# Differential attention inside a two-layer backbone: three score buffers of two banks, queries placed by transfers, norms for two heads at a time

## The chip, the cores and the metric

The kernel runs on one core of a Trainium2 chip. The metric is the device time of one execution in microseconds, the median of several runs. TensorE (PE) multiplies matrices into PSUM, which has eight banks; VectorE (DVE), ScalarE (ACT) and GpSimd (POOL) work element by element; SyncE (SP) issues the transfers. Each engine, SP's queue too, takes its instructions strictly in a fixed order and waits at one whose data or buffer is not ready.

## The reference, cut to what matters

The program is two layers of a diffusion backbone on 512 latent tokens and 256 context tokens. The change touches the differential attention of each layer, four heads, and what is computed beside it. Per head there are two softmax maps, whose difference weighs the values:

```
s = jnp.einsum("bqhmd,bkhmd->bhmqk", q, k) * (B_QK_DIM ** -0.5)      # m = 0, 1; 64 wide
p = jax.nn.softmax(s, axis=-1)
a = p[:, :, 0] - lam * p[:, :, 1]
o = jnp.einsum("bhqk,bkhd->bqhd", a, v)                               # 128 wide per head
yb = rms_norm(o, subln_g) * (1.0 - lam_init)                          # over the 128 of a head
x  = x + g1 * (concat([ya, yb, yc]) @ w_out)
```

Latent queries see all 768 keys; context queries (layer 0 alone) see the 256 context keys. The products `ya` and `yc` of two other mixers are ready before the attention starts, so that part of the product with `w_out` needs nothing of the attention.

## The kernel before, in words

Work is cut into pairs of a head and a block of 256 queries, and each pair into two units of 128 queries. Layer 0 has 4 context pairs and then 8 latent ones (24 units), layer 1 has 8 latent pairs (16 units). Per pair, `q_prep` transposes the queries on PE (tile `pq`), copies them to a rounded high part `qh` (each half of 64 rows is placed twice, by ACT and GpSimd) and subtracts on DVE for the low part `qlz` (L106). Per unit, `scores` computes for each of the two maps the product with the keys (tile `pss`, L822 with the high part, L823 with the low part), its row maximum on DVE (`mx`, L825) and the exponential on ACT (`e`). `combine` forms the difference of the maps on DVE (L841), and on GpSimd `dg` (L842), the term with the norm's epsilon. `transp` turns the result by six PE transposes (`pat`), copied to `ath` by ACT (L858, first four) and DVE (L860, last two). Per pair, `attn_v` multiplies with the values (`po`, L870), copies to `o`, squares it on ACT (`osq`) and adds `dg` on GpSimd (L875). `subln` sums the squares with a matmul by ones (`pr`, L882), takes logarithm and exponential on ACT, scales on DVE (L885) and splits into `yBh` and `yBl`.

The eight PSUM banks hold two `pss` buffers of two banks, three `w` buffers (`pq`, `pat`, `po` and `pr` take turns in them) and one `f` buffer for the filler. The filler is `wout` for the parts `ya` and `yc` (tiles `yACh`, `yACl`; PSUM tile `wo`): two chunks of weights in layer 0, three in layer 1, added to `xT` by DVE (L758). It stands last in the program, but a scheduler orders the instructions of each engine by priority and readiness, and a buffer of a pool is handed out in the order of the program.

After the fillers the main product with `w_out` follows, which reads `yBh` and `yBl`.

Of the kernel before, what the change touches and what calls it, by code (L numbers as in the profile page):

```python
# [16 lines left out]
P = 128  # L17
# [9 lines left out]
QKD = 64  # L27
# [20 lines left out]
FB, WB, EB, QB = 1, 3, 5, 3  # L48
# [28 lines left out]
def tile_backbone(  # L77
# [254 lines left out]
    for l in range(DEPTH):  # L332
# [433 lines left out]
        with ExitStack() as ph:  # L766
# [4 lines left out]

            qlz = [sp.tile([P, 2, 256], F32R, name=f"qlz{x}") for x in range(2)]
            zero = sp.tile([P, 256], F32, name="zero")
            G.memset(zero, 0.0)
            for x in qlz:
                for m in range(2):
                    ms = slice((1 - m) * QKD, (2 - m) * QKD)
                    G.tensor_copy(x[ms, m], zero[ms])
# [6 lines left out]
            def q_prep(n):  # L785
                h, p = pairs[n]
                qh = sp.tile([P, 2, 256], F32R, tag="qh", name="qh", bufs=QB)
                ql = qlz[n % 2]
                pq = ps.tile([P, 256], F32, tag="w", name="pq", bufs=WB)
                for i in range(2):  # L790
                    T.transpose(pq[:, i * P:(i + 1) * P], qt[2 * p + i][:, h * P:(h + 1) * P], ident)
                if n == 0:
                    for m in range(2):
                        for a in range(2):
                            S.copy(qh[a * QKD:(a + 1) * QKD, m], pq[m * QKD:(m + 1) * QKD])
                    for m in range(2):
                        ms = slice(m * QKD, (m + 1) * QKD)
                        sub_lo(ql[ms, m], pq[ms], qh[ms, m])
                else:
                    qn = sp.tile([P, 256], F32R, tag="qn", name="qn", bufs=2)  # L800
                    S.copy(qn, pq)
                    for m in range(2):
                        src = qn[m * QKD:(m + 1) * QKD]
                        for a in range(2):
                            (G.tensor_copy if a else S.copy)(qh[a * QKD:(a + 1) * QKD, m], src)
                    for m in range(2):
                        ms = slice(m * QKD, (m + 1) * QKD)
                        sub_lo(ql[ms, m], pq[ms], qn[ms])
                st["q", n] = (qh, ql)

            def scores(n, i):
# [17 lines left out]
                st[n, i] = (e, sm)  # L829

            def combine(n, i):
# [3 lines left out]
                if i == 0:  # L835
                    st["dg", n] = sp.tile([P, 2, P], F32, tag="dg", name="dg", bufs=3)
                dg = st["dg", n][:, i]
# [7 lines left out]
            def transp(n, i):  # L845
# [5 lines left out]
                for c0 in range(0, nk, 4):  # L851
# [5 lines left out]
                    if c0 == 0:  # L857
                        S.copy(at[osl], pat[:, :cn_])  # L858
                    else:
                        V.tensor_copy(at[osl], pat[:, :cn_])  # L860

            def attn_v(n):
# [8 lines left out]
                o = sp.tile([P, 256], F32, tag="o", name="o", bufs=2)  # L871
                sq = sp.tile([P, 256], F32, tag="osq", name="osq", bufs=2)
                S.copy(o, po)
                S.activation(sq, o, AF.Square)
                G.tensor_add(sq, sq, st["dg", n].rearrange("p a q -> p (a q)"))  # L875
                st["sub", n] = (o, sq)

            def subln(n):
                h, p = pairs[n]
                o, sq = st["sub", n]  # L880
                pr = ps.tile([P, 256], F32, tag="w", name="pr", bufs=WB)
                T.matmul(pr, ones, sq, start=True, stop=True)  # L882
# [3 lines left out]
                ts = slice(p * 256, p * 256 + 256)  # L886
                S.copy(yBh[:, h, ts], o)
                sub_lo(yBl[:, h, ts], o, yBh[:, h, ts])

            first = [(g, i) for g in whole for i in range(2)]  # L890
            if l == 0:
                w0 = wout_w(0, (0,), "pool")
                g, i = first.pop(0)
                wout(0, (0,), w0, [g], ps, "f", FB, (i,))
            q_prep(0)
            nu = len(units)
            for u in range(nu + 8):
# [15 lines left out]
                if 0 <= v < nu and units[v][1] == 1:  # L913
                    subln(units[v][0])

            for mp2 in range(NFILL[l]):
                if mp2 == 0 and l == 0:
                    for g, i in first:
                        wout(0, (0,), w0, [g], ps, "f", FB, (i,))
                else:  # L920
                    wout(mp2, (0,), wout_w(mp2, (0,), "pool"), whole, ps, "f", FB)
# [253 lines left out]
```

## Time and profile before

| | us |
|---|---|
| median of 3 runs | 1602.82 (1602.46 to 1603.99) |
| the profiled execution | 1602.73 |
| its span, first to last instruction | 1600.4 |
| PE busy in it | 1565.2 (98%) |
| DVE busy | 1016.0 (63%) |
| ACT busy | 643.3 (40%) |
| GpSimd busy | 113.3 (7%) |

The shares are means over stages that differ. The attention of layer 0 lies at about 244 to 354 us, that of layer 1 at about 1109 to 1197 us. Elsewhere after the first 100 us, PE is busy nearly without a break. A busy PE is not PE at its best: matmuls overlap, so the distance from one start to the next is what one costs in a dense row.

### The profile page before, as it was taken

Reading aid. Unit: us, or ns where it says so; the run is one execution under the profiler, and the core shown is the slowest. Engines: PE = TensorE matmul, PEld = TensorE weight load, DVE = VectorE, ACT = ScalarE, POOL = GpSimd, SP = SyncE. Lnnn points to the kernel's source line nnn. Section 1 sums busy time; section 2 is a strip of 40 time slices with the busy share of each in tenths; the row PEclk is TensorE's granted clock in tenths of the full one; section 3 lists DMA queues with packets and bytes.
Section 4 is the critical chain, followed back from the end, with each engine's and each line's share of the span. In section 5 each row is a group of like instructions: output and inputs, shape, how many; then the busy total and the mean of one; then the engine's idle time right before and its main releaser. Section 6 shows DMA issues by size and latency. Waiting matters only on the chain.

```text
span 1600.4 us, 21118 instructions
## 1 busy us (share of the span) xinstructions
PE 1565.2 (98%) x8186; PEld 1289.8 (81%) x8186; DVE 1016.0 (63%) x1713; ACT 643.3 (40%) x1115; POOL 113.3 (7%) x128
## 2 busy tenths in 40 slices
PE   6999998999999999999999999999999999999999
PEld 4875776778788888888888887887778888888888
DVE  4497968969999982145444354996977444334433
ACT  5431568762532221124333233255765333123321
POOL 1130124310000000000000000001320000000000
PEclk9999999999999999999999999999999999999999
DMA  7625210015265872116666476642011323332232
GB/s 282 216 68 183 62 54 27 14 40 198 68 196 185 284 257 74 63 66 198 209 192 207 152 272 221 202 157 93 14 42 54 103 95 96 89 103 92 92 108 90
DMA packets 76372, 208.77 MB, mean 130 GB/s; under 512 B 11504, under 2 KB 13808, under 8 KB 76144
## 3 DMA queue, kind: packets, MB, share of 16 engines
q1 hardware_dynamic: 76272, 207.43, 40.0%
q8 instruction: 64, 1.05, 0.3%
q14 instruction: 36, 0.29, 0.1%
HBM read 183.28 MB, written 24.12 MB: 130 GB/s over the span
## 4 chain that ended last, share of the span: by engine, by line
PE 91%; DVE 4%; ACT 4%; issue 1%; DMA 0%; POOL 0%; POOLq 0%; DVEq 0%; SPq 0%; ACTq 0%
PE pp L276 13%; PE pp L275 13%; PE pp L277 13%; PE pd L277 6%; PE pd L276 6%; PE pd L275 6%; PE acc L443 5%; PE acc L451 5%; PE acc L444 5%; PE po L870 3%; PE wo L275 2%; PE wo L276 2%; PE wo L277 2%; PE mr L156 2%; ACT e L97 1%; PE accC L496 1%
## 5 line engine op out<-in xcount | busy, mean ns | idle before, releaser
L220 ACT CAST whi<-raw 128x1024 fp32r<-128x1024 f32 (+1 forms) x174 | 178.4, 1027 | 510.3 <-PE pp L276 248.4
L276 PE MATMUL pp<-hlo,whi 128*128 128x512 f32 (+1 forms) x1072 | 380.6, 356 | 0.8 <-DVE hlo L316 0.8
L275 PE MATMUL pp<-hhi,whi 128*128 128x512 f32 (+1 forms) x1072 | 379.8, 356 | 1.5 <-ACT whi L220 1.3
L277 PE MATMUL pp<-hhi,wlo 128*128 128x512 f32 (+1 forms) x1072 | 379.0, 355 | 0.0
L106 DVE TENSOR_TENSOR wlo<-raw,whi 128x1024 fp32r<-128x1024 f32 (+2 forms) x159 | 191.4, 1206 | 287.9 <-ACT whi L220 280.3
L275 PEld LDWEIGHTS pp<-hhi,whi 128*128 128x128 f32 x1072 | 201.3, 188 | 35.2 <-ACT whi L220 2.7
L276 PEld LDWEIGHTS pp<-hlo,whi 128*128 128x128 f32 x1072 | 201.4, 188 | 32.8 <-DVE hlo L316 1.5
L277 PEld LDWEIGHTS pp<-hhi,wlo 128*128 128x128 f32 x1072 | 201.7, 188 | 30.9
L277 PE MATMUL pd<-gh,wlo 128*128 128x512 f32 (+1 forms) x550 | 193.2, 351 | 0.0
L276 PE MATMUL pd<-gl,whi 128*128 128x512 f32 (+1 forms) x550 | 192.5, 350 | 0.0
L275 PE MATMUL pd<-gh,whi 128*128 128x512 f32 (+1 forms) x550 | 191.8, 349 | 0.0
L275 PEld LDWEIGHTS pd<-gh,whi 128*128 128x128 f32 x550 | 103.4, 188 | 15.0
L276 PEld LDWEIGHTS pd<-gl,whi 128*128 128x128 f32 x550 | 103.3, 188 | 15.1
L277 PEld LDWEIGHTS pd<-gh,wlo 128*128 128x128 f32 x550 | 103.7, 189 | 14.4
L701 DVE SCALAR_TENSOR_TENSOR cacc<-cin,cw,cacc 128x783 f32<-128x783 f32 (+1 forms) x120 | 103.4, 913 | 3.4 <-ACT cacc L696 3.4
L1037 DVE TENSOR_TENSOR ft<-ft,pp 128x256 f32<-128x256 f32 (+1 forms) x66 | 39.4, 598 | 95.9 <-PE pp L277 84.4
L192 DVE CUSTOM_DVE_ANT_0 mraw<-mraw,csil,bmod 128x1024 f32<-128x1024 f32 x64 | 81.7, 1279 | 7.2 <-DMA mraw<-in_w_modT_dram 7.1
L97 ACT ACTIVATE ft<-ft 128x768 f32<-128x768 f32 (+1 forms) x44 | 32.6, 740 | 112.4 <-DVE ft L1032 112.3
L443 PE MATMUL acc<-whi,hhi 128*128 128x512 f32 x192 | 77.7, 405 | 0.0
L444 PE MATMUL acc<-whi,hlo 128*128 128x512 f32 x192 | 77.0, 401 | 0.0
L97 ACT ACTIVATE e<-pss,mx 128x768 f32<-128x768 f32 (+1 forms) x80 | 65.1, 816 | 16.8 <-DVE mx L825 15.0
L825 DVE TENSOR_REDUCE mx<-pss 128x1 f32<-128x768 f32 (+1 forms) x80 | 67.3, 845 | 5.6 <-PE pss L823 4.6
(218 smaller groups left out, 2522.1 us busy)
## 6 DMA issues: line engine op xcount, KB each, us to landing
raw<-in_w_gv_dram SPq DMA_DIRECT2D x88, 512.0 KB, 3.2
mraw<-in_w_modT_dram SPq DMA_DIRECT2D x64, 512.0 KB, 4.3
raw<-in_w_down_dram SPq DMA_DIRECT2D x34, 512.0 KB, 3.6
wh<-in SPq DMA_DIRECT2D x24, 512.0 KB, 4.7
wl<-in SPq DMA_DIRECT2D x24, 512.0 KB, 4.5
raw<-in_w_in_dram SPq DMA_DIRECT2D x20, 512.0 KB, 3.9
araw<-in_w_in_dram SPq DMA_DIRECT2D x40, 256.0 KB, 3.6
in<-ahi SPq DMA_DIRECT2D x40, 256.0 KB, 4.7
```

The lines of the kernel that those rows point to most:

```text
L97: r = S.activation(out, in_, func, **kw)
L106: (eng or V).tensor_sub(o, a, hi.bitcast(F32))
L192: r = V.tensor_tensor_reduce(out=junk, in0=w, in1=csil[:, s], scale=1.0, scalar=bmod[:, l, i, f:f + 1], op0=ALU.mult, op1=ALU.add, accum_o ...
L220: S.copy(hi, raw)
L275: T.matmul(o, lhi, rhi, start=start, stop=False)
L276: T.matmul(o, lhi, rlo, start=False, stop=False)
L277: T.matmul(o, llo, rhi, start=False, stop=stop)
L443: T.matmul(pt[t], hhi[hs], wh[:, a], start=k2 + a == 0, stop=False)
L444: T.matmul(pt[t], hlo[hs], wh[:, a], start=False, stop=False)
L451: T.matmul(pt[t], hhi[hs], wl[:, a], start=False, stop=k2 + 1 == KD // 2 and a == 1)
L701: V.scalar_tensor_tensor(out=cacc[:, c, :cn], in0=cin[:, c, j:j + cn], scalar=cw[:, l, c, j:j + 1], in1=cacc[:, c, :cn], op0=ALU.mult, op1 ...
L825: V.tensor_reduce(out=mx, in_=pss[:, :nk * P], op=ALU.max, axis=AX.X, negate=True)
```

## The change

- The filler's own bank goes, and the third `w` buffer; with the two banks a third `pss` buffer is made. The fillers now take turns in the two `w` buffers.
- `q_prep` makes one rounded copy on ACT and one subtraction over all 128 rows on DVE, and SP issues four transfers per pair (128 KB each) that place both parts where the matmuls want them (`qq`). The eight GpSimd copies of zeros into the `qlz` tiles and the ACT and GpSimd copies to `qh` go. The low part is now placed twice, as the high part is.
- The last two transposes' copy to `ath` goes from DVE to ACT in the second unit of each pair.
- Square, epsilon term, sum, logarithm, exponential, scaling and split run once for two heads (512 columns) instead of once per head (256).

```diff
-FB, WB, EB, QB = 1, 3, 5, 3
+WB, EB, QB = 2, 5, 3
...
-                qh = sp.tile([P, 2, 256], F32R, tag="qh", name="qh", bufs=QB)
-                ql = qlz[n % 2]
+                qq = sp.tile([P, 2, 2, 256], F32R, tag="qq", name="qq", bufs=QB)
+                qn = sp.tile([P, 2, 256], F32R, tag="qn", name="qn", bufs=2)
...
-                    S.copy(qn, pq)
-                    for m in range(2):
-                        src = qn[m * QKD:(m + 1) * QKD]
-                        for a in range(2):
-                            (G.tensor_copy if a else S.copy)(qh[a * QKD:(a + 1) * QKD, m], src)
-                    for m in range(2):
-                        ms = slice(m * QKD, (m + 1) * QKD)
-                        sub_lo(ql[ms, m], pq[ms], qn[ms])
+                S.copy(qn[:, 0], pq)
+                sub_lo(qn[:, 1], pq, qn[:, 0])
+                for m in range(2):
+                    for a in range(2):
+                        nc.sync.dma_start(out=qq[a * QKD:(a + 1) * QKD, :, m].bitcast(F32), in_=qn[m * QKD:(m + 1) * QKD].bitcast(F32))
...
-                    pss = ps.tile([P, 1024], F32, tag="s", name="pss", bufs=2)
+                    pss = ps.tile([P, 1024], F32, tag="s", name="pss", bufs=3)
...
-                    if c0 == 0:
+                    if c0 == 0 or i == 1:
                         S.copy(at[osl], pat[:, :cn_])
...
-                S.copy(o, po)
+                if n % 2 == 0:
+                    st["sub", n // 2] = sp.tile([P, 2, 256], F32, tag="o", name="o", bufs=2)
+                S.copy(st["sub", n // 2][:, n % 2], po)
+
+            def subln(x):
...
+                sq = sp.tile([P, 2, 256], F32, tag="osq", name="osq", bufs=2)
                 S.activation(sq, o, AF.Square)
...
+                G.tensor_add(sq, sq, st["dg", x])
+                T.matmul(pr.rearrange("p y q -> p (y q)"), ones, sq.rearrange("p y q -> p (y q)"), start=True, stop=True)
...
-                wout(0, (0,), w0, [g], ps, "f", FB, (i,))
+                wout(0, (0,), w0, [g], ps, "w", WB, (i,))
...
-                    wout(mp2, (0,), wout_w(mp2, (0,), "pool"), whole, ps, "f", FB)
+                    wout(mp2, (0,), wout_w(mp2, (0,), "pool"), whole, ps, "w", WB)
```

Three places show how the order moves. The first is PE's order in layer 0 where the attention of the kernel before is under way, among the latent units (`pss` scores, `pat` transposes, `pq` query transposes, `wo` filler):

```order
L109 MATMUL pat<-ident,e 128x128
L791 MATMUL pq<-ident,q_1269 128x128
L791 MATMUL pq<-ident,q_1270 128x128
L277 MATMUL wo<-yACh,wlo 128x512
L275 MATMUL wo<-yACh,whi 128x512
L276 MATMUL wo<-yACl,whi 128x512
```

The second is the end of the attention of layer 0 in PE's order after the change (`po` values, `pr` the sum of squares for two heads):

```order
L852 MATMUL po<-ath,vt 128x256 x6
L865 MATMUL pr<-osq,ones 128x512
L275 MATMUL wo<-yACh,whi 128x256
L276 MATMUL wo<-yACl,whi 128x256
L277 MATMUL wo<-yACh,wlo 128x256
```

Before, filler matmuls stand between the attention's in many places. After, every filler but the first group of 12 in layer 0 stands behind the last `pr`, in both layers.

The third is the start of the attention of layer 0 in PE's order, behind the first three query transposes, first before the change:

```order
L275 MATMUL wo<-yACh,whi 128x256
L276 MATMUL wo<-yACl,whi 128x256
L277 MATMUL wo<-yACh,wlo 128x256
L822 MATMUL pss<-kk,qh 128x256
L275 MATMUL wo<-yACh,whi 128x256
```

And after it, with the row of SP's queue in which the transfers of the queries stand apart:

```order
L785 MATMUL pq<-ident,q_1273 128x128
L785 MATMUL pq<-ident,q_1274 128x128
L804 MATMUL pss<-kk,qq 128x256
L805 MATMUL pss<-kk,qq 128x256
```

```order
L790 DMA qq<-qn 64x2x256 x48
```

The filler between the first transposes and the first scores is gone, and the first scores now stand behind transfers. On SP's queue the 48 transfers of layer 0 stand in one run behind the loads of `w_out` and ahead of the weight loads of the next stage; layer 1 has 32 in the same way.

## Rows read from the trace of the kernel before

**Rows 1.** The page: busy us, share of the span and instructions of each engine.

```profile
PE 1565.2 (98%) x8186; PEld 1289.8 (81%) x8186; DVE 1016.0 (63%) x1713; ACT 643.3 (40%) x1115; POOL 113.3 (7%) x128
```

**Rows 2.** Windows: stretch, length, busy us by engine, granted clock, DMA share, GB/s.

```profile
600.00:700.00 100.00, 100.00 (x571) 87.47 (x571) 26.97 (x34) 14.91 (x16) 0.00 (x0) 1.00 0.23 71
```

**Rows 3.** Windows: first row maximum's start to the last one's end, layers 0, 1.

```profile
247.21:339.55 92.34, 82.99 (x448) 67.95 (x446) 84.53 (x176) 74.32 (x195) 33.96 (x57) 0.96 0.03 10
1112.06:1181.75 69.69, 65.69 (x355) 53.77 (x354) 65.30 (x120) 53.73 (x124) 24.61 (x35) 1.00 0.03 9
```

**Rows 4.** Waits of PE, layer 0: us in total, times, longest.

```profile
PE pss L822 <- ACT e L97: 5.7, 8, 1.1
```

**Rows 5.** Waits of DVE in the first stretch of rows 3.

```profile
DVE mx L825 <- PE pss L823: 3.0, 7, 1.0
DVE cc L838 <- ACT e L97: 2.6, 5, 1.1
```

**Rows 6.** DVE by line and shape, layer 0: count, busy us, mean ns, idle before.

```profile
L106 DVE TENSOR_TENSOR qlz<-pq,qn 64x256 fp32r<-64x256 f32 x22 | 9.2, 418 | 0.4
L885 DVE SCALAR_TENSOR_TENSOR o<-o,gsub,osq 128x256 f32<-128x256 f32 x12 | 7.1, 594 | 2.9 <-ACT osq L97 2.8
L860 DVE COPY ath<-pat 128x256 f32<-128x256 f32 x16 | 6.5, 413 | 1.7 <-PE pat L109 1.6
...
L758 DVE SCALAR_TENSOR_TENSOR xT<-wo,modv,xT 128x512 f32<-128x512 f32 x4 | 3.0, 744 | 0.4 <-PE wo L277 0.3
L106 DVE TENSOR_TENSOR wlo<-raw,whi 128x1024 fp32r<-128x1024 f32 x2 | 2.5, 1226 | 0.9 <-ACT whi L220 0.9
```

**Rows 7.** Timeline at both attentions' starts: start, us, engine, instruction.

```profile
244.28 0.82 PE L791 MATMUL pq<-ident,q 128*128 128x128 f32 x6
...
243.15 2.39 POOL L106 TENSOR_TENSOR wlo<-raw,whi 128x1024 fp32r<-128x1024 f32 x1 [2.56 <-ACT vt L731]
...
1108.79 0.82 PE L791 MATMUL pq<-ident,q 128*128 128x128 f32 x6
```

**Rows 8.** Transfers: count, KB each, median us from issue to landing.

```profile
in<-araw SPq DMA_DIRECT2D x40, 256.0 KB, 4.9
...
out_dram<-xT SPq DMA_DIRECT2D x4, 128.0 KB, 1.8
```

**Rows 9.** ACT by line and shape, layer 0.

```profile
L858 ACT COPY ath<-pat 128x512 f32<-128x512 f32 x16 | 9.3, 582 | 3.5 <-PE pat L109 3.3
...
L858 ACT COPY ath<-pat 128x256 f32<-128x256 f32 x8 | 3.0, 371 | 0.9 <-PE pat L109 0.9
```

**Rows 10.** Timeline behind the last row maximum, layer 0 and then layer 1.

```profile
348.10 0.73 POOL L875 TENSOR_TENSOR osq<-osq,dg 128x256 f32<-128x256 f32 x1 [3.78 <-ACT osq L874]
...
348.89 0.70 PE L882 MATMUL pr<-osq,ones 128*128 128x256 f32 x2 [0.41 <-POOL osq L875]
...
353.81 0.28 PE L275 MATMUL wo<-yBh,whi 128*128 128x256 f32 x1
...
1191.32 0.70 PE L882 MATMUL pr<-osq,ones 128*128 128x256 f32 x2 [0.71 <-POOL osq L875]
1191.67 0.58 PE L275 MATMUL wo<-yACh,whi 128*128 128x512 f32 x1
...
1197.32 0.40 PE L275 MATMUL wo<-yBh,whi 128*128 128x512 f32 x1
```

**Rows 11.** Windows of 2 us in the context units of layer 0.

```profile
248.00:250.00 2.00, 0.95 (x4) 0.59 (x4) 1.88 (x7) 1.67 (x7) 1.51 (x4) 1.00 0.05 20
...
254.00:256.00 2.00, 1.20 (x5) 1.24 (x6) 0.97 (x4) 1.79 (x7) 1.24 (x3) 0.50 0.00 0
```

**Rows 12.** Timeline, one DVE form twice, and GpSimd beside the first.

```profile
259.39 0.68 DVE L841 SCALAR_TENSOR_TENSOR e<-e,cc 128x256 f32<-128x256 f32 x1
...
261.45 0.47 DVE L841 SCALAR_TENSOR_TENSOR e<-e,cc 128x256 f32<-128x256 f32 x1
...
259.77 0.62 POOL L842 TENSOR_SCALAR dg<-epsi,sm 128x128 f32<-128x128 f32 x1
```

More of the change, by code (lines that the diff above doesn't have):

```diff
@@ L770, in tile_backbone @@
             V.tensor_scalar_mul(gsub, sublt[:, l:l + 1], 1.0 - lam0)
[L772 to L775, printed above, removed]
-                for m in range(2):
-                    ms = slice((1 - m) * QKD, (2 - m) * QKD)
-                    G.tensor_copy(x[ms, m], zero[ms])
             pairs = [(h, p) for p in range(2) for h in range(HEADS)]
@@ L791, in q_prep @@
                     T.transpose(pq[:, i * P:(i + 1) * P], qt[2 * p + i][:, h * P:(h + 1) * P], ident)
[L792 to L809 removed]
+                S.copy(qn[:, 0], pq)
[3 more added lines that the diff above has]
+                        nc.sync.dma_start(out=qq[a * QKD:(a + 1) * QKD, :, m].bitcast(F32), in_=qn[m * QKD:(m + 1) * QKD].bitcast(F32))
+                st["q", n] = (qq[:, 0], qq[:, 1])
             def scores(n, i):
@@ L834, in combine @@
                 cc = sp.tile([P, 1], F32, tag="cc", name="cc", bufs=4)
-                if i == 0:
-                    st["dg", n] = sp.tile([P, 2, P], F32, tag="dg", name="dg", bufs=3)
-                dg = st["dg", n][:, i]
+                if i == 0 and n % 2 == 0:
+                    st["dg", n // 2] = sp.tile([P, 2, 256], F32, tag="dg", name="dg", bufs=3)
+                dg = st["dg", n // 2][:, n % 2, i * P:(i + 1) * P]
                 V.reciprocal(out=cc, in_=sm[:, 1:2])
@@ L870, in attn_v @@
                     T.matmul(po, vt[:, kt, hs], at[:, c], start=c == 0, stop=c == nk - 1)
-                o = sp.tile([P, 256], F32, tag="o", name="o", bufs=2)
-                sq = sp.tile([P, 256], F32, tag="osq", name="osq", bufs=2)
-                S.copy(o, po)
-                S.activation(sq, o, AF.Square)
[L875 to L882, printed above, removed]
+                if n % 2 == 0:
+                    st["sub", n // 2] = sp.tile([P, 2, 256], F32, tag="o", name="o", bufs=2)
+                S.copy(st["sub", n // 2][:, n % 2], po)
+            def subln(x):
+                h, p = pairs[2 * x]
+                o = st["sub", x]
+                sq = sp.tile([P, 2, 256], F32, tag="osq", name="osq", bufs=2)
+                S.activation(sq, o, AF.Square)
+                pr = ps.tile([P, 2, 256], F32, tag="w", name="pr", bufs=WB)
+                G.tensor_add(sq, sq, st["dg", x])
+                T.matmul(pr.rearrange("p y q -> p (y q)"), ones, sq.rearrange("p y q -> p (y q)"), start=True, stop=True)
                 act(sq, pr, AF.Ln, scale=1.0 / P)
@@ L885, in subln @@
                 V.scalar_tensor_tensor(out=o, in0=o, scalar=gsub, in1=sq, op0=ALU.mult, op1=ALU.mult)
-                ts = slice(p * 256, p * 256 + 256)
-                S.copy(yBh[:, h, ts], o)
-                sub_lo(yBl[:, h, ts], o, yBh[:, h, ts])
+                osl = (slice(None), slice(h, h + 2), slice(p * 256, p * 256 + 256))
+                S.copy(yBh[osl], o)
+                sub_lo(yBl[osl], o, yBh[osl])
             first = [(g, i) for g in whole for i in range(2)]
@@ L912, in tile_backbone @@
                 v = u - LAG[2]
-                if 0 <= v < nu and units[v][1] == 1:
-                    subln(units[v][0])
+                if 0 <= v < nu and units[v][1] == 1 and units[v][0] % 2 == 1:
+                    subln(units[v][0] // 2)
             for mp2 in range(NFILL[l]):
@@ L918, in tile_backbone @@
                     for g, i in first:
-                        wout(0, (0,), w0, [g], ps, "f", FB, (i,))
+                        wout(0, (0,), w0, [g], ps, "w", WB, (i,))
                 else:
-                    wout(mp2, (0,), wout_w(mp2, (0,), "pool"), whole, ps, "f", FB)
+                    wout(mp2, (0,), wout_w(mp2, (0,), "pool"), whole, ps, "w", WB)
         kvs.close()
```

## The prediction

> **What bounds the kernel now.** I read the page's shares first: PE is busy 98% of the span [rows 1]. The windows then show where this holds: between the attentions PE is busy 100.00 of 100 us [rows 2], so nothing there can be gained by the other engines. The change lies in the two attentions alone, so the windows around them come next, cut from the start of the first row maximum to the end of the last [rows 3]. There DVE is busy 84.5 of 92.3 us in layer 0 and 65.3 of 69.7 us in layer 1, PE 83.0 and 65.7, ACT 74.3 and 53.7. The attention runs at DVE's pace, and PE's gaps beside it are stuffed with filler. The waits tell what is left: PE waits 5.7 us for the exponential to free one of the two score buffers [rows 4], and DVE waits 3.0 us for scores and 2.6 us for the exponential [rows 5]. Last I read how each attention starts and ends in the timeline [rows 7, 10].
>
> So the ledger of one layer has four entries: (A) from the query transposes to the first row maximum, (B) from the first to the last maximum, (C) from there to the end of the last sum of squares `pr`, (D) from there to the main product, which reads `yBh`. All times are of the profiled execution (1602.73 us, within 0.1 us of the median).
>
> **The change part by part.**
>
> *B, work taken from DVE.* In layer 0 the 24 subtractions over 64 rows at 0.42 us [rows 6] (two of them read another tile) become 12 over 128 rows; the same columns per row, so I put them at 0.42 us each: -5.0. Of 16 `ath` copies 8 go to ACT: -3.3. Twelve scalings of 0.594 us become six, put at the 0.744 us of the same kind of operation on 512 columns: -2.6. The splits into `yBl` halve in count and double in columns: about 0. The fillers' additions to `xT` and the weight split `wlo` leave this stretch with the fillers; a part of them stood behind it already, so of 3.0 us on 512 columns, as much again on 256, and 2.5 us I take -3.7. Sum 14.6; neighbouring DVE rows overlap by a tenth or so and a little of this lies behind the last maximum, so 12 of 84.5 us. In layer 1 the same arithmetic (16 units, no context) gives 9.5 of 65.3.
>
> What becomes of DVE's idle time, 7.8 and 4.4 us in B? The third score buffer takes away the wait of rows 4. Against it stands the loss of the third `w` buffer: a transposed block, the values' product and the query transposes of the next pair now share two, and PE, in order, waits for a copy by ACT or DVE at nearly each change of hands. I let the two cancel and keep the idle time in microseconds: B is -12 and -9.5. Bounds: DVE never idle, 12.2 us better in both layers together; its idle time doubled, 12.2 us worse. ACT is no bound: it loses the `qh` casts and half of the norm's fixed parts and gains 8 copies of 0.371 us [rows 9] per layer.
>
> *A, queries by transfer.* Before, the first scores used ACT's casts at once. Now: transposes at 244.28 [rows 7], some 0.25 us for the first two; ACT's cast (a copy of this size takes 0.37 [rows 9]), DVE's subtraction 0.42, and hand-overs: ready at 245.6. SP's queue has a load of `w_out` in front that waits for GpSimd's split at 243.15 + 2.39 = 245.54, so the transfers issue at about 245.9. No transfer of this kind is in the trace; the nearest by size lands in 1.8 us (128 KB), the slowest pair of the kind in 4.9 us (256 KB to memory) [rows 8]. I take 2.2, near the row of the same size, as four go at once. With the scores, the first maximum stands at 248.7 instead of 247.21: +1.5, bounds +1.1 and +4.2. Layer 1, from 1108.79, gives +1.4. Later pairs are prepared a pair ahead, some 8 us, which hides up to 4.9 us; the context pairs, half as long, are hidden only just. Behind the transfers on SP stand only loads of the next stage.
>
> The Trainium skill (DMA: Bandwidth & Descriptors, "Anatomy of one DMA — SWDGE (gpsimd) path") puts a fixed cost of about 2.0 us on a transfer of GpSimd's path, bytes coming on top; the 128 KB of rows 8, issued by SP, landed in 1.8 us all told. By the page 128 KB would be an estimated 2.3 us, and A would be +1.6.
>
> *C, the tail.* The last pair's chain after the exponential stays, but its links are twice as wide: the square +0.2 (371 to 582 ns [rows 9]), GpSimd's addition +0.7 (0.73 us on 256 columns [rows 10]; at most doubled), `pr` +0.4 of 0.70. +1.3 per layer; if the longer links cost nothing, 0.
>
> *D, the fillers.* This is the large one. All the filler but one group now stands behind the last `pr` on PE. Its rate in a dense row: 24 matmuls on 512 columns from 1191.67 to 1197.32 [rows 10], 0.235 us each, and half of that on 256 columns. Layer 0 has 36 on 256 and 48 on 512 columns: 4.2 + 11.3 = 15.5 us; layer 1 has 72 on 512: 16.9 us. Before, from the end of the last `pr` (348.89 + 0.70) to the main product (353.81) it took 4.2 us, in layer 1 (1191.32 + 0.70 to 1197.32) 5.3 us. So D is +11.3 and +11.6. What it hides, the norm of the last heads and the split of the next weights, was hidden before.
>
> *Clock.* In layer 0 the granted clock falls to 0.50 (1.2 of 2.4 GHz) at 254 to 256 after PE was busy 0.95 of 2 us at 248 to 250 [rows 11]. Without filler both attentions start with a gap of some 3 us on PE. Layer 0 has such a dip already; for a new one in layer 1 I add 1.5, bounds 0 and 5 for all places.
>
> Sum: layer 0 +1.5 -12 +1.3 +11.3 = +2.1; layer 1 +1.4 -9.5 +1.3 +11.6 = +4.8; clock +1.5. Together +8.4: 1602.7 + 8.4 = 1611.1, **1611 us**. In words: the change buys about as much from DVE as the filler then costs behind it, and pays for the wider tail and the later start.
>
> **The rivals.**
>
> *R1, faster: three score buffers and a lighter DVE make the attention run without gaps.* For it: the largest single wait of PE is for a score buffer [rows 4], and DVE's two waits of rows 5 are both of this chain. Price: all 12.2 us of DVE's idle time, 1611.1 - 12.2 = 1598.9. It decides from the point where B in the two layers together has shrunk by 30 us instead of 21.5. Against it: it asks for an in-order DVE without any gap while PE, ACT and DVE are all above three quarters busy. It has a second source: one DVE operation took 0.68 us beside a GpSimd operation and 0.47 us alone [rows 12], and the change removes the GpSimd copies to `qh`; a dozen such, 0.2 us each, are 2.5 us per attention. The Trainium skill (SBUF — State Buffer, "Who interferes with whom") says that a DVE instruction with two SBUF inputs contends with a GpSimd one that reads SBUF; the rows agree, by 0.2 us.
>
> *R2, the two `w` buffers bind.* Each pair asks for five or six of them. Where 16 latent pairs wait some 0.6 us more (about half of the longest wait of rows 4) for a copy behind an exponential on ACT, B grows by 10 us: 1621. For it: PE's own matmuls now fill the shorter stretch as tightly as attention and filler together filled it before. Against it: the order puts scores between two uses of a buffer.
>
> *R3, the transfers are late.* At 4.9 us each start is 2.7 us later, and the four context pairs, with about 4 us of lead, wait some 1.5 us each: +11, 1622. Against it: the DMA engines are nearly idle here, a share of 0.03 [rows 3].
>
> *R4, no change.* DVE's relief and the fillers meet within the noise, with no dip of the clock and half of DVE's idle time gone: 1611.1 - 1.5 - 6.1 = 1603.5.
>
> **How the numbers follow.** Forecast 0.45, R1 0.11, R2 0.20, R3 0.10, R4 0.14. A measurement of this kernel can tell about 0.2%, 3.2 us, from no change. Faster is R1: 0.11. Same is R4: 0.14. Slower is the rest: 0.75. The forecast's own range, from the bounds of A, C and the clock and a quarter of DVE's idle time either way, is 1606 to 1618. For eight in ten I go from 1601, between R4 and R1, to 1624, just above R2 and R3.
>
> **What would show it.** Right: in the changed trace no `wo` matmul stands between the scores of layer 1; some 15 and 17 us of dense `wo` rows follow the last `pr`; first to last maximum is 80 and 60 us; the first maximum comes 1.5 us later after the transposes. R1 shows as 73 and 56 us there, R2 as PE waits of `pat` and `po` for ACT above 10 us, R3 as PE waits of `pss` for DMA. What would make me wrong is above all entry B: it is worked out from DVE's work, and three engines share its pace.

## The result and the profile of the changed kernel

The changed kernel takes 1626.77 us (median of 4 runs, 1625.44 to 1628.17), the kernel before 1602.88 us beside it: 1.0148 times as long, 95% interval 1.013 to 1.0166. The forecast was slower, 1611 us, with an eight-in-ten range that ended at 1624; the loss is 23.9 us instead of 8.4.

The page's line of PE, and then the windows of the two stretches from the first row maximum's start to the last one's end, layer 0 and layer 1 (columns as in [rows 3]):

```profile
PE 1573.1 (97%) x8166; PEld 1292.1 (80%) x8166; DVE 998.6 (62%) x1657; ACT 626.9 (39%) x1049; POOL 86.5 (5%) x72
...
250.95:336.58 85.63, 75.33 (x374) 59.62 (x375) 71.25 (x142) 63.49 (x160) 19.96 (x28) 0.90 0.29 66
1129.28:1189.12 59.84, 55.53 (x296) 44.08 (x296) 54.08 (x94) 45.86 (x103) 11.79 (x18) 0.98 0.25 57
```

DVE lost the work that it was to lose (84.5 to 71.3 us, 65.3 to 54.1), ACT and GpSimd lost work too. But PE did 20 instructions fewer in 7.9 us more of busy time than in [rows 1]: part of them ran at a lower clock. The granted clock is 0.90 in the first stretch, 0.96 before.

The start of layer 0 and of layer 1 in the timeline (start, duration, engine, instruction, in brackets the idle time before it and what ended it):

```profile
244.05 0.38 PE L785 MATMUL pq<-ident,q 128*128 128x128 f32 x2
...
245.69 9.57 SPq L790 DMA_DIRECT2D qq<-qn  x12
...
250.14 0.55 PE L804 MATMUL pss<-kk,qq 128*128 128x256 f32 x1 [4.36 <-DMA qq<-qn]
...
1122.56 0.60 PE L785 MATMUL pq<-ident,q 128*128 128x128 f32 x4
...
1127.75 0.64 PE L804 MATMUL pss<-kk,qq 128*128 128x512 f32 x1 [3.42 <-DMA qq<-qn]
```

The transfers are issued from 245.69 on, as forecast (245.9), but the first scores start 4.45 us later. They read two of the four transfers of their pair, and SP issues these one after the other. The rows of the first transfer, of the second with what waited for it, and of all 80 (duration of the issue in ns, minimum, median and maximum; then the landing):

```profile
L790 SPq DMA_DIRECT2D qq<-qn x1: 658/658/658, 245.7 to 245.7; - x1
DMA to landing us min/median/max: 3.7/3.7/3.7
...
L790 SPq DMA_DIRECT2D qq<-qn x1: 612/612/612, 246.4 to 246.4; - x1
  PE pss L804: 4.4, 1
DMA to landing us min/median/max: 3.6/3.6/3.6
...
L790 SPq DMA_DIRECT2D qq<-qn x80: 590/607/1487, 245.7 to 1177.4; - x80
DMA to landing us min/median/max: 2.3/2.4/4.0
```

So the 4.45 us are 0.7 us until the second transfer is issued, 3.6 us until it has landed, and 0.1 us to the scores. Over the whole program the median landing is 2.4 us.

The Trainium skill (DMA: Bandwidth & Descriptors, "Anatomy of one DMA — SWDGE (gpsimd) path") would give, by its fit for GpSimd's path, an estimated 2.3 us for 128 KB. The median agrees; the first landing, 3.7 us with a `w_out` load of 512 KB (issued at 245.31) and the next transfers under way beside it, does not.

PE's clock behind that start (windows of 2 us: length, PE busy, granted clock, DMA share, GB/s):

```profile
246.00:248.00 2.00, 0.00 (x0) 0.81 0.70 256
248.00:250.00 2.00, 0.00 (x0) 0.50 0.91 261
...
254.00:256.00 2.00, 1.00 (x5) 0.50 0.88 198
...
262.00:264.00 2.00, 2.00 (x9) 0.50 0.89 200
264.00:266.00 2.00, 1.10 (x6) 0.92 0.11 23
```

From 247.3 to 264.3 us the granted clock is 0.50, 1.2 of 2.4 GHz; before, this lasted 6.8 us around [rows 11]. Two shorter stretches follow, the second in layer 1. All three as windows, and then the one of the kernel before:

```profile
247.30:264.30 17.00, 10.92 (x40) 0.50 0.55 138
271.10:274.55 3.45, 3.45 (x9) 0.51 0.63 143
1127.90:1131.30 3.40, 3.40 (x11) 0.50 0.66 153
```

```profile
252.50:259.30 6.80, 5.72 (x24) 0.50 0.00 0
```

PE was busy at 0.50 for 17.8 us instead of 5.7; half of the difference, 6.0 us, is an estimate of what this cost. Idle time ended by scores has grown as well. DVE's waits of [rows 5] and PE's of [rows 4] read, in layer 0 from the query transposes on:

```profile
DVE mx L807 <- PE pss L805: 16.8, 15, 4.9
...
PE pss L804 <- ACT e L97: 5.2, 11, 1.1
PE pss L804 <- DMA qq<-qn: 5.0, 3, 4.4
```

So the third score buffer did not take away PE's wait for the exponential (5.7 us before). Of DVE's 16.8 us the longest wait, 4.9, is the one for the first scores and belongs to entry A below; that leaves 11.9 us in B, where it was 3.0. The ends of the two layers, which answer to [rows 10]:

```profile
346.70 1.26 POOL L864 TENSOR_TENSOR osq<-osq,dg 128x512 f32<-128x512 f32 x1 [8.18 <-ACT osq L862]
...
348.01 1.12 PE L865 MATMUL pr<-osq,ones 128*128 128x512 f32 x2 [2.51 <-POOL osq L864]
...
366.62 0.28 PE L275 MATMUL wo<-yBh,whi 128*128 128x256 f32 x1
...
1200.56 1.12 PE L865 MATMUL pr<-osq,ones 128*128 128x512 f32 x2 [2.52 <-POOL osq L864]
...
1220.59 0.40 PE L275 MATMUL wo<-yBh,whi 128*128 128x512 f32 x1
```

From these rows the four entries of the prediction's ledger, before, after, the difference, and what was forecast for it:

| us | before | after | difference | forecast |
|---|---|---|---|---|
| layer 0, A | 2.93 | 6.90 | +4.0 | +1.5 |
| B | 92.34 | 85.63 | -6.7 | -12 |
| C | 10.03 | 12.56 | +2.5 | +1.3 |
| D | 4.22 | 17.48 | +13.3 | +11.3 |
| layer 1, A | 3.27 | 6.72 | +3.5 | +1.4 |
| B | 69.69 | 59.84 | -9.9 | -9.5 |
| C | 10.27 | 12.56 | +2.3 | +1.3 |
| D | 5.30 | 18.90 | +13.6 | +11.6 |

The differences sum to +22.5 us of the 23.3 by which the spans differ. The same two stretches, from the query transposes to the main product, as PE's own account; before, then after (length, PE busy, clock):

```profile
244.28:353.81 109.53, 98.78 (x531) 0.97 0.03 10
1108.79:1197.32 88.53, 83.59 (x437) 1.00 0.07 25
```

```profile
244.05:366.62 122.57, 103.36 (x519) 0.92 0.29 76
1122.56:1220.59 98.03, 86.24 (x430) 0.98 0.24 60
```

This view I should have read first. PE has the same products to do in both kernels (12 and 7 records fewer, the `pr` that now take two heads at once). Layer 0 is longer by 13.0 us: 8.5 us more in which PE is idle (10.75 to 19.21), and 4.6 us more of busy time for the same work. Layer 1 is longer by 9.5 us: 6.9 us idle (4.94 to 11.79) and 2.65 us more of busy time. The lower clock accounts for most of the busy time's growth, 4.3 and 1.7 us by the estimate above, but not for all of it: with the banks alone (first run below) layer 1 shows as much growth at a clock of 1.00, and no run separates the cause.

```profile
1117.62:1215.91 98.29, 86.16 (x437) 1.00 0.06 19
```

With 76 and 60 filler matmuls ahead of the last `pr`, PE was the engine with the least to spare (DVE is idle 16.5 and 12.0 us in the same stretches before), and whatever leaves it idle or slow sets the time.

### The profile page after: what moved, and what is told of

It is laid out like the page before. It is cut to its first block, busy times and chain, and to the rows that moved or that the text cites. A ratio compares the mean times of both kernels' runs of the same rounds, so it can differ in the third digit from the quotient of the medians.

```text
span 1623.7 us, 21043 instructions
## 1 busy us (share of the span) xinstructions
PE 1573.1 (97%) x8166; PEld 1292.1 (80%) x8166; DVE 998.6 (62%) x1657; ACT 626.9 (39%) x1049; POOL 86.5 (5%) x72
## 4 chain that ended last, share of the span: by engine, by line
PE 90%; DVE 4%; ACT 3%; DMA 1%; issue 1%; POOL 0%; SPq 0%; DVEq 0%; ACTq 0%; POOLq 0%
PE pp L276 13%; PE pp L275 13%; PE pp L277 13%; PE pd L275 6%; PE pd L277 6%; PE pd L276 6%; PE acc L443 5%; PE acc L451 5%; PE acc L444 5%; PE po L852 3%; PE wo L275 2%; PE wo L277 2%; PE wo L276 2%; PE mr L156 2%; PE pss L804 1%; PE accC L495 1%
## 5 line engine op out<-in xcount | busy, mean ns | idle before, releaser
L804 PE MATMUL pss<-kk,qq 128*128 128x256 f32 (+1 forms) x144 | 58.9, 416 | 17.3 <-ACT e L97 8.7
```

## The experiments

Theory 1: the loss is the place of the filler. Behind the last `pr` it takes PE's full time, and the gaps it left are idle and, in part, lower the clock; the other parts of the change matter little. Rival, theory 2 in most runs: another part (transfers, buffers, a wider norm) costs it. All runs, with their differences from the kernel before on the same chip; the last columns are length, PE idle and clock from the first query transposes to the main product, in the one execution that was profiled:

| run | us | difference | ratio, 95% | layer 0 | layer 1 |
|---|---|---|---|---|---|
| banks alone | 1620.70 | +18.3 | 1.0102 to 1.013 | 117.5, 14.4, 0.94 | 98.3, 12.1, 1.00 |
| transfers alone | 1600.03 | -2.4 | 0.9977 to 0.9995 | 108.2, 12.0, 1.00 | 87.6, 4.8, 1.00 |
| paired norms alone | 1607.01 | +4.6 | 1.0019 to 1.0037 | 111.0, 12.1, 0.97 | 90.3, 5.9, 0.98 |
| `ath` copies alone | 1599.65 | -2.7 | 0.9975 to 0.9992 | 108.4, 8.5, 0.95 | 87.7, 4.2, 1.00 |
| all but the banks | 1603.36 | +0.6 | 0.9993 to 1.0011 | 110.8, 13.8, 0.99 | 89.0, 6.1, 1.00 |
| filler in four `w` | 1626.24 | +23.5 | 1.0133 to 1.016 | 123.2, 20.6, 0.93 | 99.0, 13.0, 0.98 |
| two `w`, two filler | 1610.49 | +7.9 | 1.0027 to 1.0054 | 111.7, 12.8, 0.98 | 93.3, 7.6, 0.98 |
| changed, filler spread | 1615.13 | +12.8 | 1.0068 to 1.0093 | 110.3, 13.5, 0.98 | 100.1, 12.5, 0.97 |
| spread, gaps filled | 1606.51 | +4.3 | 1.0018 to 1.0037 | 109.7, 11.3, 0.98 | 91.6, 6.1, 1.00 |
| changed, filler at start | 1622.48 | +19.7 | 1.0113 to 1.0144 | 115.7, 17.9, 0.99 | 98.0, 11.7, 0.98 |
| changed, extra matmuls | 1625.84 | +23.2 | 1.0131 to 1.0159 | 122.9, 16.3, 0.94 | 98.6, 9.3, 1.00 |
| changed, first pair cast | 1622.52 | +20.2 | 1.0104 to 1.0135 | 124.3, 18.7, 0.92 | 98.3, 10.2, 0.97 |
| changed, 2 KB runs | 1628.38 | +25.6 | 1.0142 to 1.017 | 121.6, 19.7, 0.93 | 100.0, 11.3, 0.95 |
| transfers + copies | 1602.55 | +0.2 | 0.9992 to 1.001 | 106.4, 10.6, 1.00 | 92.4, 6.8, 0.96 |
| the same, filler held | 1602.23 | 0.0 | 0.999 to 1.0008 | 107.5, 10.7, 1.00 | 88.9, 5.3, 1.00 |
| held, paired norms | 1602.36 | +0.1 | 0.9991 to 1.0009 | 108.5, 11.6, 1.00 | 87.9, 5.3, 1.00 |
| transfers, copies, pairs | 1600.46 | -1.9 | 0.9981 to 0.9998 | 108.8, 12.5, 1.00 | 87.5, 5.2, 1.00 |

**The four parts, each alone in the kernel before.** The edits are those of the change's diff; for the banks:

```diff
-FB, WB, EB, QB = 1, 3, 5, 3
+WB, EB, QB = 2, 5, 3
...
-                    pss = ps.tile([P, 1024], F32, tag="s", name="pss", bufs=2)
+                    pss = ps.tile([P, 1024], F32, tag="s", name="pss", bufs=3)
...
-                    wout(mp2, (0,), wout_w(mp2, (0,), "pool"), whole, ps, "f", FB)
+                    wout(mp2, (0,), wout_w(mp2, (0,), "pool"), whole, ps, "w", WB)
```

> The kernel before with the banks alone changed: three score buffers, two `w` buffers, the fillers in `w`. Theory 1 (the filler's place costs most): all filler stands behind the last `pr`, entry D grows by about 13 us in each layer, and the shorter stretch of maxima (fillers' additions to `xT` gone, wait for a score buffer gone) gives back about 8 us in each; 1602.8 + 26 - 16 = 1613 us. Theory 2 (the transfers and the clock cost most, the banks repay themselves): the stretch of maxima shrinks by as much as D grows, 1604 us or less. Rival of the prediction R2 (two `w` buffers bind): the stretch of maxima doesn't shrink at all, 1628 us.

> The kernel before with the query split and placement alone changed (one cast, one subtraction over 128 rows, four transfers), three `w` buffers and the filler beside the scores as before. Theory 1: the start of each layer is late by 3.4 to 4 us, DVE's 5 us of saved subtractions give back some 3 us in each layer, filler keeps PE and its clock up meanwhile; 1604 us. Theory 2: transfers and the clock are most of the loss; 1615 us or more, with the granted clock at 0.50 for over 15 us at the start of layer 0.

> The kernel before with the norm for two heads at a time alone. Theory 1: the last chain is longer by 2.3 to 2.5 us in each layer, hidden in part by the filler that still stands there, and DVE's six saved scalings give back some 2 us in each; 1603 us, no change. Theory 2 (the wider chain costs in full, DVE's saving is worth nothing): 1607.5 us.

> The kernel before with the second block's copy to `ath` on ACT instead of DVE alone, 8 per layer. Theory 1 (DVE sets the pace of the attentions): 3.3 us less of DVE work per layer, some 2.5 us of it in time; 1598 us. Theory 2 (DVE, PE and ACT share the pace, ACT now does it later behind its exponentials): 1602 to 1604 us.

The banks cost 18.3 us by themselves, the transfers gain 2.4, the norms cost 4.6 and the copies gain 2.7. For the banks that is theory 1, 8 us dearer than it said; the transfers are 4 us better than theory 1 and far from theory 2; the norms cost what theory 2 said; the copies are near theory 1. The four sum to +17.9; all together cost +23.9, so 6 us arise only between them. Where: with the banks alone layer 0 is 8.0 us longer and layer 1 9.8; with the whole change 13.0 and 9.5. The 6 us lie in layer 0, where the four sum to some +7 us (in layer 1 to +9.9). The transfers alone start the maxima nearly as late as the whole change does (6.5 us behind the transposes, 6.9 there), but filler runs meanwhile. Windows of the transfers alone and then of the banks alone:

```profile
248.00:250.00 2.00, 1.16 (x6) 1.00 0.89 263
...
254.00:256.00 2.00, 2.00 (x13) 1.00 0.67 154
```

```profile
244.00:246.00 2.00, 1.22 (x6) 1.00 0.12 14
246.00:248.00 2.00, 1.76 (x8) 0.71 0.70 248
248.00:250.00 2.00, 1.49 (x6) 0.50 0.00 0
...
254.00:256.00 2.00, 1.53 (x7) 0.50 0.00 0
```

With the transfers and filler the clock stays at 1.00, though PE was busy only 1.16 of the 2 us from 248 on; with the banks alone it has fallen by then, even with the casts that bring the queries early. Filler beside the scores does not always hold it: the kernel before and the copies alone have filler there and fall to 0.50 at 252.5 and 250.5 us.

**The banks taken apart.** First the filler alone is moved to the end: it takes its buffers from `w`, of which there are now four (`FB, WB = 1, 3` becomes `WB = 4`, and `"f", FB` becomes `"w", WB`), with two score buffers as before. Then only one `w` buffer is taken away and given to the filler (`FB, WB = 2, 2`). Last, the changed kernel gets the old banks back.

> The kernel before with two score buffers as it had, and the filler taking its buffers from `w`, of which there are now four: all 96 and 84 matmuls stand behind the last `pr`, but no use of `w` is short of buffers. Theory 1 (the filler's place is the cost): entry D grows by 12 to 15 us in each layer and the stretch of maxima gives back some 5 us in each, 1618 us or more, near the 1620.7 us of the banks alone. Theory 2 (two `w` buffers instead of three are the cost): 1602 to 1608 us.

> The kernel before with one `w` buffer given to the filler: two `w` buffers instead of three, two filler buffers instead of one, two score buffers as before. The filler stands among the scores (84 and 72 matmuls before the last `pr`, 12 behind it). Rival R2 of the prediction (two `w` buffers bind the attention): the stretch of maxima grows by 10 us, 1612 us or more. Theory 1 (two are enough; the filler's place was the loss): 1600 to 1604 us.

> The changed kernel with the banks of before put back (two score buffers, three `w` buffers, the filler's own bank); transfers, paired norms and the `ath` copies stay. Filler stands beside the scores again (84 and 72 matmuls between the first query transposes and the last `pr`, 12 behind it). Theory 1 (the parts add up except that late queries without filler let the clock fall): 1602.4 - 2.4 + 4.6 - 2.7 = 1602 us, and no row of layer 0's start at a clock of 0.50. Theory 2 (the transfers disturb whatever stands beside them): over 1610 us.

The filler's place alone costs 23.5 us, nearly as much as the whole change, as theory 1 had it. A buffer of `w` goes out in the program's order, and the filler is written last; so no filler matmul can start before the last `pr` has its buffer, whatever the scheduler would like. The windows of the stretch of maxima show why nothing comes back for it:

```profile
247.30:337.45 90.15, 76.49 (x398) 63.12 (x397) 80.98 (x171) 73.47 (x195) 32.53 (x57) 0.92 0.02 5
1125.50:1191.95 66.45, 56.71 (x306) 46.57 (x304) 60.90 (x114) 51.24 (x121) 18.72 (x35) 0.97 0.00 1
```

Without filler the stretch is only 2.2 and 3.2 us shorter than in [rows 3]. The filler had used time of PE that the attention leaves open in any case, at a cost of these few us at most. With the banks alone (two `w` buffers, three for scores, filler behind as well) the time is 5.5 us less than this, so the third score buffer is worth more there than two `w` buffers. The second run costs 7.9 us with the filler in place, and both its theories missed: it is less than the prediction's rival R2 said, and it is not nothing. Its edit does two things, though. With a second buffer the filler is also used up sooner (84 and 72 matmuls between the first transposes and the last `pr`, 76 and 60 before), and at each layer's end PE then runs 3.4 us at 0.50, where before it ran at 1.00. So 7.9 us is the price of the exchange, and the share of the missing `w` buffer is not separated. With the old banks back the change costs 0.6 us, within the interval of no change, as theory 1 had it.

**The filler written back among the units.** Buffers as in the changed kernel, the order of the program altered:

```diff
+            if l == 0:
+                filler(2)
             nu = len(units)
...
+                if u >= 4 and u % (3 if l == 0 else 2) == 0:
+                    with low(0):
+                        filler()
                 v = u - LAG[0]
```

Here `filler(n)` issues the next n groups of 12 matmuls.

> The changed kernel, its buffers as they are (three for scores, two `w`), with the filler's groups written between the units of the attention instead of behind them: two groups behind the first query transposes of layer 0, the rest one at a time every third unit (layer 0) or second unit (layer 1). 84 and 72 filler matmuls then stand between the first query transposes and the last `pr`, 12 behind it. Theory 1 (the place of the filler and the clock that falls without it are the loss): most of the 24 us come back, 1604 us, entry D some 2 and 3.5 us, no row of layer 0's start below 0.9. Theory 2 (two `w` buffers bind once filler asks for them as well): scores wait for the filler's turn at `w`, the stretch of maxima grows to 92 and 70 us, 1613 us or more.

Layer 0 returned to 110.3 us, layer 1 did not (100.1). The time, 1615.13 us, is the one that theory 2 named; the stretch of maxima grew as it said in layer 1 (75.4 us) and not in layer 0 (88.5 us). The rows of layer 1 show two places where PE stood without work and the clock fell behind it; this is the second, at the end (4 us windows from 1196 on, and the row of `pr`):

```profile
1203.50 2.07 PE L865 MATMUL pr<-osq,ones 128*128 128x512 f32 x2 [3.57 <-POOL osq L864]
```

```profile
1200.00:1204.00 4.00, 0.50 (x1) 0.94 0.40 132
1204.00:1208.00 4.00, 4.00 (x11) 0.63 0.38 134
```

The next run puts a group into each of these gaps (`filler(2 if l == 0 else 1)` behind the first query transposes, the last group between the last `po` and its `pr`) and so has fewer left for the units: one every fourth unit in layer 0 and every third in layer 1, instead of every third and second.

> The changed kernel with the filler spread as in the earlier run, and one group more of it placed where PE stood idle: in layer 1 one group behind the first query transposes, in both layers one group between the values' product of the last head and its `pr`. Theory 1 (in the attentions PE's own work is the bound, and what counts is its idle time and the half clock behind each long gap): the gaps of 3.4 us (start of layer 1) and 3.6 us (last `pr`) are filled, the clock stays at 0.9 or more in every 4 us of layer 1, PE's idle time there falls from 12.5 to some 6 us, and the time from 1615.1 to 1605 us. Theory 2 (the two `w` buffers, now asked for by filler too, are what holds the stretch of layer 1): the clock stays up but the idle time moves to other places, 1612 us or more.

Theory 1: PE's idle time in layer 1 falls from 12.5 to 6.1 us, the clock is 1.00, the stretch 8.5 us shorter, and the time 8.6 us less. The idle time did not move elsewhere, as theory 2 had it; that fewer groups stand between the units may have helped as well, which this run does not separate. So 20 of the 24 us come back with the changed kernel's buffers, by the order of the filler alone. PE's account of layer 1, first without, then with the gaps filled:

```profile
1108.80:1208.90 100.10, 87.57 (x430) 0.97 0.28 74
```

```profile
1109.20:1200.80 91.60, 85.49 (x429) 1.00 0.28 74
```

**The start of layer 0.** Four edits of the changed kernel: three filler groups behind the first query transposes (`for g, i in first[:3]: wout(...)` behind `q_prep(0)`); 20 extra matmuls there instead (`T.matmul(pd, identr, kk[:, 0, :512], ...)`); the first pair placed by casts and subtractions (`if n == 0`); and the `qq` tile with the two parts of a map side by side (`qq[a * QKD:(a + 1) * QKD, m]`).

> The changed kernel with three more filler groups of layer 0 (12 matmuls on 256 and 24 on 512 columns) written behind the first query transposes, so that they run while the first queries are on their way. Theory 1: PE has work through the landing, the clock stays at 1.00 at the start of layer 0 (some 6 us back), and 7 us of filler leave entry D for a gap that was idle, less 2 to 3 us by which the first scores start later; 1626.6 - 6 - 7 + 2.5 = 1616 us. Theory 2 (the clock falls for the thin work behind the start, not for the gap): the clock is at 0.50 there all the same, and the time is 1621 us.

> The changed kernel with 20 extra matmuls on 512 columns, whose product is not used, behind the first query transposes of each layer: some 4.7 us of work that fills the wait for the first transfers and nothing else (the filler stays behind the last `pr`). Theory 1 (the gap on PE makes the clock fall, and that costs): the clock at layer 0's start stays near 1.00, PE's busy time from the first query transposes to the main product, less the extra 4.7 us, falls by some 4 us, and the kernel gains 3 to 5 us although it has more to do, 1622 us. Theory 2 (the thin work behind the start makes it fall, as with the banks alone, where the gap was short): the fall comes later but comes, 1626 us or more.

> The changed kernel with the first pair of heads of each layer placed by ACT's casts and DVE's subtractions, without transfers; every later pair as it was. Theory 1 (the late first queries cost in full because no filler covers them): entry A shrinks by 3 to 4 us in each layer, and with the clock of layer 0's start still falling to 0.50 for want of filler (as it did with the banks alone) the time is 1619 to 1621 us. Theory 2 (the gap for the landing is what makes the clock fall): A shrinks and the clock stays at 1.00 in layer 0, 1614 us or less.

> The changed kernel with the queries' tile laid out so that high and low part of one map lie together: each transfer writes 2 KB runs instead of 1 KB runs, the same bytes. Theory 1 (the first transfers wait for the DMA engines, which are at a share of 0.9 then, and packets of 1 KB make them slow): the first landing falls by over 1 us, 1623 us or less. Theory 2 (the landing is a matter of bytes and of the `w_out` load beside it): the first landing stays within 0.5 us and the time within 2 us of 1626.6.

The filler at the start took layer 0 from 122.6 to 115.7 us with the clock at 0.99, theory 1's way. But this is the fastest of four executions, 1618.58 to 1625.3 us, with a mean clock of 0.994 over the program and 0.988 to 0.993 in the others; their median is 4 us less than the changed kernel's, nearer to theory 2's number. The extra matmuls filled the gap, yet the clock fell behind it. Windows of that run:

```profile
246.00:248.00 2.00, 2.00 (x10) 1.00 0.68 242
...
252.00:254.00 2.00, 0.53 (x3) 1.00 0.31 71
...
256.00:258.00 2.00, 2.00 (x9) 0.50 0.89 200
```

So the gap before the first scores is not the whole cause: theory 2 was right on the fall, and the time is the changed kernel's (-0.9 us). In layer 1, where the same matmuls fill the gap, the clock stays at 1.00 (0.98 in the changed kernel). The Trainium skill (TensorE: Matmul & The Clock Gate, "HAM oscillation — how this bites in real kernels") says that idle gaps of PE bring it back to half clock. The end of layer 1 with the filler spread (above) and with transfers and copies (below) shows that here. At the start of layer 0 shorter gaps did it too: with the banks alone PE was idle 0.8 us of the 2 us from 244 on and 0.2 of the next 2, and the clock had begun to fall.

With the first pair cast, entry A shrank by 4.4 and 3.9 us, but the clock fell all the same (0.92) and D grew; 4 us were gained where 6 to 8 were expected. This run does not settle whether the gap makes the clock fall, since the gap only moved: PE now waits for the second pair's transfers, and from 248 to 250 us it was busy 0.35 of 2 us.

```profile
249.97 0.55 PE L811 MATMUL pss<-kk,qq 128*128 128x256 f32 x1 [1.65 <-DMA qq<-qn]
```

The execution profiled is also the slowest of four (1626.25 us at a mean clock of 0.988; the fastest took 1618.67 at 0.995). Runs of 2 KB instead of 1 KB changed nothing: PE waited 4.75 us for its first queries instead of 4.36, the median landing stayed 2.4 us, and theory 2 held.

**Whether the gains add.** The kernel before with transfers and `ath` copies, then the same with the last filler group of each layer held for the last `pr` (from `w`, written between the last `po` and `pr`), then with paired norms except for the last two heads, held and not held:

> The kernel before with only the two parts of the change that won by themselves: queries split once and placed by transfers, and the second block's `ath` copy on ACT; banks and single-head norms as before. Theory 1 (the two gains are of different DVE work and add): 1602.4 - 2.4 - 2.7 = 1597.3 us. Theory 2 (ACT, which takes the copies, is then the engine that the next link waits for, and the gains share one limit): 1599.5 us.

> The kernel of the transfers and the `ath` copies, with the last filler group of each layer held back (12 matmuls, from a `w` buffer) so that it stands between the values' product of the last head and its `pr`. Theory 1 (the two gains failed to add because faster attentions ran out of filler at their end, PE stood idle there and the clock fell to 0.50 over the rest of the filler in layer 1): no row of layer 1 below 0.9, entries C and D of layer 1 shrink from 17.5 to some 14 us, and the sum of the two gains comes out, 1597 us. Theory 2 (the gains share one limit elsewhere): 1601 us or more.

> As the run before, and with norms for two heads at a time except for the last two heads of each layer. Theory 1 (PE's idle time and clock are the limit): PE idles no less for fewer DVE and ACT instructions, and the time is within 1.5 us of the run before. Theory 2 (DVE's and ACT's work still sets the pace): 2 to 3 us below it.

> The kernel of the transfers and the `ath` copies, with norms for two heads at a time except for the last two heads of each layer, which are done singly as before. Theory 1 (the paired norm lost only through its wider chain at each layer's end, 2.8 and 4.9 us in entry C, and won 1.8 and 3.3 us of the stretch of maxima): the gain alone stays, 3 to 5 us below the kernel of the transfers and the `ath` copies, 1593 us. Theory 2 (the pair's norm comes a head later and in one lump, and that costs within the stretch as much as it saves): no change against it.

Gains of 2.4 and 2.7 us gave none together. In layer 1 the faster attention ran out of filler, PE waited 3.69 us at its end, and the rest ran at half clock:

```profile
1192.46 1.22 PE L865 MATMUL pr<-osq,ones 128*128 128x256 f32 x2 [3.69 <-POOL osq L858]
```

```profile
1188.00:1192.00 4.00, 0.77 (x4) 0.90 0.11 15
1192.00:1196.00 4.00, 3.54 (x8) 0.50 0.73 247
```

With a group held for that place the clock is 1.00 and layer 1 is 3.5 us shorter, as theory 1 said; but layer 0 became 1.1 us longer and the median fell by only 0.3 us, not by 5. There theory 1 missed. In the kernels with filler beside the scores, old banks and no half clock at the ends, both layers together take 195.8 (transfers), 196.1 (copies, with 10 us at half clock at layer 0's start), 196.3, 196.4 and 196.4 us: whatever DVE, ACT or GpSimd lost, some 196 us remain (why just these is not shown; DVE's busy time in the two layers is 169.6 us before and 155.4 and 153.4 in the two kernels with a group held, and the length falls from 198.1 by less than 2 us), with the transfers alone 179.0 us of PE's work at a clock of 1.00 and 16.8 us of its idle time. That the paired norms change nothing there (1602.36 beside 1602.23) is theory 1 again. The run without a held group, 1600.46, fits neither number that was written for it. Of all versions the `ath` copies alone have the lowest median, 1599.65 us, 0.1 to 0.25% below before and 27 us below the changed kernel; the transfers alone are within 0.4 us of it. Why kernels with equal stretches differ by 2 us in their medians I can't tell from these runs.

## Why the prediction was wrong

The direction, and the change's two large entries (B and D), were right in kind; the sum was nearly 16 us short. By its own steps:

- **D** was forecast at +11.3 and +11.6 and measured +13.3 and +13.6. The 12 matmuls on `yACh` and `yACl` of the main product, which stand before the first that reads `yBh`, were left out: 12 x 0.12 us in layer 0, 12 x 0.23 in layer 1. What remains is below 1 us.
- **B** held in layer 1 (-9.9 for -9.5) and failed in layer 0 (-6.7 for -12). DVE's lost work was 13.3 and 11.2 us for 12 and 9.5; what failed is "I let the two cancel and keep the idle time". DVE's idle time in B rose from 7.8 to 14.4 us in layer 0, with 11.9 us of waits for scores, and from 4.4 to 5.8 in layer 1, where two misses met and the number came out by luck. The wait of rows 4 did not go (5.2 us). Scores came from a PE at half clock from 247 to 264 us, and exchanging a `w` buffer cost 7.9 us in a run of its own; how much of the 5.3 us each of the two took was not separated.
- **A** was +4.0 and +3.5 for +1.5 and +1.4. Landing was taken at 2.2 us, from the row of the same size, "as four go at once". They do not: SP issued the second 0.7 us behind the first, and it landed after 3.6 us. The bound of +4.2 held that value.
- **C** was +2.5 and +2.3 for +1.3. GpSimd's addition (+0.5 for +0.7), `pr` (+0.4) and the square (+0.2) grew about as said; the last `po` starts 1.4 us later behind the last maximum (6.1 us instead of 4.7), and in the trace the norm of the pair of heads before it, now of double width, stands around the last `ath` copies on ACT. The banks have a part as well: C is 11.7 us in both layers with the banks alone, and 9.2 and 10.5 us with four `w` buffers, the filler behind in both runs.
- **Clock**, put at 1.5 us with a bound of 5 for all places: PE's surplus of busy time is 7.2 us, of which 6.0 are the clock's by the estimate above. "Layer 0 has such a dip already" was read as cover; the dip there went from 6.8 to 17.0 us, and two of 3.4 us came in addition. What the clock took lies in A to D, so it is no entry beside them.

The misses of A to D, 4.6, 4.9, 2.2 and 4.0 us, less the 1.5 us booked for the clock, are the 14 us by which the two stretches exceed the 8.4 us forecast; the rest of the gap lies outside them and between profiled executions and medians.

Behind the sizes stands one error of method: the sum was made against DVE as the bound, with PE's 83.0 of 92.3 us read as slack. With its filler PE had only 10.75 and 4.94 us of idle time in the two layers, and so gains on other engines could bring about these at most, plus the clock's 3 us (half of 5.7); the change instead raised them to 19.2 and 11.8. R1 and R4 are refuted. R2's sign was not seen: PE's waits of `pat` and `po` for ACT in B, weight loads included, are some 7 us in layer 0 and 3 us in layer 1, not above 10; the exchange of buffers is a real cost below its price and did not decide. R3's delay came for the first pair of each layer (+4.0 and +3.5 for its +4.2), by a shorter landing behind a second issue; later pairs were all but hidden, with 0.6 us of waits in layer 0's B.

## What to carry to other kernels

Where filler is to run beside a bound stage, the pool that it draws its buffers from is part of its place: a buffer handed out in program order pins the filler behind everything that is written before it and draws from the same pool. Before summing what other engines save, take PE's busy and idle time and its clock over the whole stretch, filler included: here that idle time bounded what could be won, and filler moved behind the stretch shortened it by only 2.2 and 3.2 us. Keep a piece of filler for the places where the chain of the last unit leaves PE without work, since the half clock behind such a gap also slows the row that follows.

## What the runs showed of the hardware

- SP issued the 80 transfers of 128 KB between SBUF tiles one at a time, each issue taking 0.6 us (median); they landed 2.4 us after issue (median, 2.3 to 4.0). The first two, beside a 512 KB load, took 3.7 and 3.6 us. Doubling the run length from 1 to 2 KB left the median at 2.4.
- From 248 to 250 us the granted clock stood at 1.00 with PE busy 1.16 us (transfers alone), and at 0.50 with PE busy 1.49 us (banks alone, where it had fallen before). Once at 0.50 it stayed there through windows in which PE was busy all of 2 us (262 to 264 us of the changed kernel).
